# Last tokens' low parts on VectorE, a projection between halves of the modulation's matmuls, and a second modulation group on VectorE

## The chip, the cores and the metric

The kernel runs on one core of a Trainium2 chip. The metric is device time in microseconds. The kernel before took 2394.74 us (median of three executions, 2394.31 to 2396.17). A core has TensorE (matmuls; PE in the profile, its weight loads PEld), VectorE (DVE), ScalarE (ACT), GpSimd (POOL) and SyncE (SP, which issues the DMAs here). Each runs its own queue in order; semaphores join them.

## The reference, cut to what matters

Two layers of a diffusion backbone over 512 latent and 128 context tokens, 1024 wide. Each token's normalised input is scaled and shifted by a modulation that is computed from a conditioning vector and a large matrix `w_mod` (1024 x 6144 for each layer); there are two conditioning vectors, one for latent and one for context tokens.

```python
mod = matmul(silu(cond), w_mod) + b_mod
sh1, sc1, ga1, sh2, sc2, ga2 = split(mod, 6)
h = rmsnorm(x, g_pre1) * (1 + sc1) + sh1
proj = matmul(h, w_in)                 # 12 pieces: four mixers' inputs and the gates
br = einsum('btmc,mcd->btmd', branches, w_br)   # a, b, c, d: attention, MLA, pooling, gated DeltaNet
mix = matmul(sum(sigmoid(gate) * br), w_o)
x = x + ga1 * rmsnorm(mix, g_post1)
h2 = rmsnorm(x, g_pre2) * (1 + sc2) + sh2
gt, up = split(matmul(h2, w_up), 2)
x = x + ga2 * rmsnorm(matmul(silu(gt) * up, w_down), g_post2)
```

## The kernel before

The 640 tokens are five tiles of 128 (`NT` is 5): tiles 0 to 3 latent, tile 4 context. Nearly every matmul is done in three products of rounded halves: an operand v is split into a high part (ScalarE copies it to the rounded type) and a low part (v minus the high part, a subtraction of two SBUF operands, on VectorE or GpSimd); then high x high, high x low and low x high go into one PSUM bank. Weights come in chunks through `wchunk` (lines 139 to 150 for the call): DMA into `raw`, ScalarE makes `whi`, VectorE makes `wlo` at line 150. All matmuls of this kind are recorded at line 134, transposes at line 139.

A scheduler with priorities orders each engine's queue when the kernel is built; `after` and `keep` bind one instruction behind another on the same engine; pools of named slots (`V` 2, `P` 4, `U` 4, `raw`, `whi`, `wlo` 3 each) and PSUM banks (`psg` 3, `pss` 2, `psc`, `pst`, `pso` 1 each) make a later user wait for the earlier one. So an edit at one place can move instructions at others.

Layer 0 fills the span up to about 1205 us, its feed-forward from about 760; layer 1 follows, its feed-forward from about 1940. What the change touches:

*The normalised tile before the feed-forward.* `prenorm` transposes tile i, scales it (line 371 on VectorE, 369 on ScalarE), and then, for the feed-forward, `norm_blocks` makes the parts by halves q of the model width. High parts come from ScalarE at line 1280; the low part of half 0 is on GpSimd, that of half 1 on VectorE, both at line 1282. The tokens go to two blocks of 320 tokens; `U` holds both parts of a block's first half, `hhi`/`hlo` those of its second half. `combine` (line 1293 and its ScalarE copies at 1297) then makes sums of blocks, into `X` and `T`, for a scheme that saves one of the products of the up projection. Ahead of the attention layers, `prenorm` itself makes the parts (line 377), in the same split of engines.

*The first projection.* At the start of layer 0 the modulation itself (`first_norm`, line 417, 32 matmuls for a chunk of 256 columns of shift and scale, small moving operand, weights straight from DMA) and the projection `proj_tm` run together: a chunk's modulation, and then the projection of the chunk before it, for five token tiles, six products each.

*The other modulation groups.* A group is 2048 columns of `w_mod`. `mod_group` does one on TensorE (line 207, 32-column weights, blocks from `V`), as a generator `bg` that the gates and projections of a layer advance. `mod_group_v` does one on VectorE: 64 multiply-adds of 128x512 (line 308 the first of an accumulator, line 310 the others, 8 DMAs for each of 4 accumulators of tag `P`), then 8 matmuls with a selecting matrix and `mod_finish`, with 4 transposes. It is the feed-forward's `filler`; `step()` advances it by one piece (two DMAs, four multiply-adds). Layer 0 has groups 1 and 2 on TensorE; for layer 1, group 0 is the filler in layer 0's feed-forward, and groups 1 and 2 are on TensorE in layer 1.

*The feed-forward.* `ffn` takes the 22 blocks of hidden columns in six groups (`FGROUPS`); in each, up projections of pairs of blocks, the gating, the split of the hidden values into `U`, and a `w_down` pass whose results are added into `acc` and `oh` at line 1472. Products of transformed operands bring subtractions at line 1323.

## Time and profile before

| | |
|---|---|
| median of three | 2394.74 us |
| the profiled execution | 2396.94 us |
| its span, first to last instruction | 2395.1 us |
| mean granted TensorE clock | 0.989 |
| PE busy | 2291.1 us (96%) |
| PEld busy | 2020.9 us (84%) |
| DVE busy | 1577.0 us (66%) |
| ACT busy | 984.2 us (41%) |
| POOL busy | 280.5 us (12%) |
| DMA, mean over the span | 113 GB/s |

Busy times are summed for each engine over the span. A timeline row has the start of an instruction, its duration, the engine, the line of the kernel, the operation with the tile it writes and those it reads, partitions by elements, and in brackets how long the engine had been idle before it and which engine's result ended that. Durations of neighbours overlap, so what one costs in a run of equal ones is the distance between their starts. A row marked x4 stands for four such instructions in sequence. A row of the windows view has a stretch, its length, the busy time of PE, PEld, DVE, ACT and POOL in it with the count of instructions, the granted TensorE clock, the busy share of the DMA engines and GB/s. A granted clock of 1.00 is 2.4 GHz, 0.50 is 1.2 GHz.

### The profile page before, as it was taken

The page shows a single profiled execution, that of the slowest core. Times are in us where ns is not written, and L with a number is a line of the kernel's source. Part 1 is how long each engine was busy: PE and PEld are TensorE (multiplying, and loading weights), DVE is VectorE, ACT ScalarE, POOL GpSimd, SP SyncE. Part 2 cuts the span into 40 slices and gives each one's busy share as a digit, 9 for nine tenths or more (in the row PEclk, how much of TensorE's full clock was granted, in tenths as well). Part 3 has the DMA queues.
Part 4 walks back from the last instruction along what each step waited for, and adds up shares of the span by engine and source line. Part 5 has one row for each costly group of instructions (what it writes and reads, how often), then busy time and mean ns, then how long its engine had stood idle before and what let it go on. Part 6 is the DMA issues. An engine that isn't in the chain of part 4 may idle for free. (4 is left out here: it accounts for less than half of the span.)

```text
span 2395.1 us, 38984 instructions
## 1 busy us (share of the span) xinstructions
PE 2291.1 (96%) x15094; PEld 2020.9 (84%) x15094; DVE 1577.0 (66%) x3370; ACT 984.2 (41%) x2046; POOL 280.5 (12%) x326
## 2 busy tenths in 40 slices
PE   7999999999999899999989999999999979999998
PEld 5877678989887889998878776889798869999997
DVE  5562787567357898666766538884763577667667
ACT  3351444233226534433564424532322355334433
POOL 0100113223022100000020002031310320000001
PEclk9999999999999999999999999999999989999999
DMA  8637213414434344222452561334253432223223
GB/s 263 168 118 214 68 58 99 126 51 111 134 127 140 98 134 141 78 71 93 121 154 73 157 205 30 99 85 100 60 137 124 129 123 71 88 72 106 71 89 114
DMA packets 328330, 269.48 MB, mean 113 GB/s; under 512 B 71552, under 2 KB 287232, under 8 KB 328144
## 3 DMA queue, kind: packets, MB, share of 16 engines
q1 hardware_dynamic: 328144, 266.98, 37.4%
q8 instruction: 119, 1.95, 0.3%
q14 instruction: 67, 0.55, 0.1%
HBM read 234.73 MB, written 32.20 MB: 111 GB/s over the span
## 5 line engine op out<-in xcount | busy, mean ns | idle before, releaser
L134 PE MATMUL psg<-hhi,whi 128*128 128x384 f32 (+2 forms) x1648 | 515.9, 320 | 11.7 <-DVE tg L1175 5.6
L134 PE MATMUL psg<-hhi,wlo 128*128 128x384 f32 (+2 forms) x1648 | 512.7, 318 | 2.2 <-DVE wlo L150 2.0
L134 PE MATMUL psg<-hlo,whi 128*128 128x256 f32 (+2 forms) x1568 | 504.0, 321 | 0.1
L150 DVE TENSOR_TENSOR wlo<-raw,whi 128x1024 fp32r<-128x1024 f32 (+1 forms) x176 | 219.5, 1248 | 208.2 <-ACT whi L149 205.5
L134 PEld LDWEIGHTS psg<-hhi,whi 128*128 128x128 f32 x1648 | 310.7, 190 | 22.9 <-DVE tg L1175 7.1
L134 PEld LDWEIGHTS psg<-hhi,wlo 128*128 128x128 f32 x1648 | 310.8, 190 | 15.5 <-issue 9.3
L134 PEld LDWEIGHTS psg<-hlo,whi 128*128 128x128 f32 x1568 | 298.2, 190 | 15.6 <-issue 13.2
L149 ACT ACTIVATE whi<-raw 128x1024 fp32r<-128x1024 f32 (+1 forms) x176 | 185.7, 1057 | 225.1 <-PE psg L134 166.6
L1144 ACT ACTIVATE tg<-psg 128x384 f32<-128x384 f32 (+1 forms) x128 | 54.9, 431 | 222.0 <-PE psg L134 203.1
L1337 ACT ACTIVATE wlo<-raw 128x512 fp32r<-128x512 f32 x120 | 75.8, 632 | 158.2 <-PE psc L134 91.4
L1323 DVE TENSOR_TENSOR wlo<-raw,wlo 128x512 fp32r<-128x512 f32 x120 | 82.8, 690 | 64.8 <-ACT wlo L1337 64.2
L134 PE MATMUL pss<-hhi,whi 128*128 128x320 f32 x504 | 122.9, 309 | 0.0
L134 PE MATMUL pss<-hhi,wlo 128*128 128x320 f32 x504 | 122.7, 308 | 0.0
L134 PE MATMUL psg<-oh,whi 128*128 128x384 f32 (+1 forms) x512 | 117.7, 315 | 3.8 <-DVE tg L1175 3.5
L134 PE MATMUL psg<-whi,U 128*128 128x512 f32 x356 | 118.7, 393 | 1.8 <-DVE U L157 1.3
L1177 POOL TENSOR_TENSOR acc<-acc,tg 128x640 f32<-128x640 f32 x48 | 85.3, 1780 | 241.8 <-DVE tg L1175 241.8
L1488 POOL TENSOR_TENSOR acc<-acc,oh 128x512 f32<-128x512 f32 x8 | 11.3, 1409 | 814.4 <-ACT dt L1487 808.4
L1323 DVE TENSOR_TENSOR whi<-raw,whi 128x512 fp32r<-128x512 f32 x120 | 82.3, 689 | 33.9 <-ACT whi L1337 33.9
L134 PE MATMUL pss<-whi,U 128*128 128x512 f32 x304 | 102.4, 391 | 0.8 <-DVE cv L1323 0.8
L134 PEld LDWEIGHTS psg<-oh,whi 128*128 128x128 f32 x512 | 85.0, 188 | 14.2 <-DVE tg L1175 6.9
L1337 ACT ACTIVATE whi<-raw 128x512 fp32r<-128x512 f32 x120 | 75.4, 631 | 41.5 <-DVE raw L1323 27.4
L134 PEld LDWEIGHTS pss<-hhi,whi 128*128 128x128 f32 x504 | 87.3, 188 | 0.0
(578 smaller groups left out, 5114.6 us busy)
## 6 DMA issues: line engine op xcount, KB each, us to landing
raw<-in_w_up SPq DMA_DIRECT2D x88, 512.0 KB, 3.6
raw<-in_w_in SPq DMA_DIRECT2D x86, 512.0 KB, 3.8
V<-in_w_mod SPq DMA_DIRECT2D x64, 512.0 KB, 4.7
raw<-in_w_down SPq DMA_DIRECT2D x44, 512.0 KB, 3.7
raw<-in_w_o SPq DMA_DIRECT2D x16, 512.0 KB, 3.8
V<-in_w_mod SPq DMA_DIRECT2D x32, 256.0 KB, 2.7
xs<-V SPq DMA_DIRECT2D x15, 512.0 KB, 3.4
V<-xs SPq DMA_DIRECT2D x15, 512.0 KB, 3.5
```

The lines of the kernel that those rows point to most:

```text
L134: return self.nc.tensor.matmul(out, lhsT, rhs, start=start, stop=stop, skip_group_check=True)
L149: nc.scalar.activation(hi, raw[:, :a * b], AF.Copy)
L150: nc.vector.tensor_tensor(lo, raw[:, :a * b], hi, op=ALU.subtract)
L1144: self.nc.scalar.activation(tg[:, o:o + sz], p, AF.Tanh, scale=0.5)
L1177: nc.gpsimd.tensor_tensor(a, a, tg, op=ALU.add)
L1323: tt = lambda o, x, y, op: nc.vector.tensor_tensor(o, x, y, op=op)
L1337: nc.scalar.activation(hi, src, AF.Copy)
L1488: nc.gpsimd.tensor_tensor(y, y, G[0 if i < 4 else 1][:, 0:512], op=ALU.mult)
```

## The change

Three edits. First, in `prenorm` and `norm_blocks` the low part of half 0 is on GpSimd for tiles 0 to 2 only; for tiles 3 and 4 it is on VectorE. Second, in `proj_tm` a chunk's modulation matmuls are bound in two halves; the previous chunk's projection of tile 0 stands between the halves, that of tile 1 behind the second, ahead of the transpose. Third, group 1 of layer 1's modulation goes from TensorE in layer 1 to VectorE in layer 0's feed-forward, behind group 0, and `step()` is called once more for each chunk of `w_down`.

```diff
--- before.py
+++ after.py
@@ -373,7 +373,7 @@
             if which:
                 continue
             nc.scalar.activation(hh[0][:, ks, sl], h32[:, ks], AF.Copy)
-            eng = nc.gpsimd if q == 0 else nc.vector
+            eng = nc.gpsimd if q == 0 and i < 3 else nc.vector
             eng.tensor_tensor(hh[1][:, ks, sl], h32[:, ks], hh[0][:, ks, sl], op=ALU.subtract)
         if which:
             self.norm_blocks(i, h32, hh)
@@ -515,17 +515,21 @@
         if norm:
             for c in range(4):
                 mods = next(norm)
+                n = len(mods) // 2
                 if prev:
                     self.after(mods[0], prev[-1])
                 chs[c] = self.tm_chunk(l, c)
                 tr = next(norm)
                 if c:
+                    prev.append(mods[n - 1])
+                    part(c - 1, range(1))
+                    self.after(mods[n], prev[-1])
                     prev.append(mods[-1])
-                    part(c - 1, range(1))
+                    part(c - 1, range(1, 2))
                 self.after(tr, prev[-1] if prev else mods[-1])
                 prev.append(tr)
                 if c:
-                    part(c - 1, range(1, NT))
+                    part(c - 1, range(2, NT))
             part(3, range(NT))
         else:
             for c in range(2):
@@ -1278,7 +1282,7 @@
                 hi, lo = hb[3 * q if second else 1 + q]
                 v = h32[:, 4 * q:4 * q + 4, src]
                 nc.scalar.activation(hi[:, :, dst], v, AF.Copy)
-                eng = nc.gpsimd if q == 0 else nc.vector
+                eng = nc.gpsimd if q == 0 and i < 3 else nc.vector
                 eng.tensor_tensor(lo[:, :, dst], v, hi[:, :, dst], op=ALU.subtract)
 
     def combine(self, i, h32, hb):
@@ -1462,6 +1466,7 @@
                     ps = [self.ps(b) for b in ("ssctg" if half == 0 else "ggssc")]
                     for k in range(0, nf, 2):
                         ch = mk(k, co)
+                        step()
                         for i in range(NT):
                             self.tmm(ps[i], ch, (0, 1), hs, (k, k + 1), i, k == 0, k == nf - 2)
                     for i in range(NT):
@@ -1533,7 +1538,7 @@
             br = {}
             br[2] = self.mixer_c(l, hh, L)
             br[0] = self.mixer_a(l, hh, L, tm)
-            self.bg = chain(*(self.mod_group(M, g, "c", "c") for g in (1, 2)))
+            self.bg = chain(*(self.mod_group(M, g, "c", "c") for g in ((1, 2) if l == 0 else (2,))))
             G = self.gdn_scalars(L, ab)
             if l == 0:
                 zt = self.t("X", [128, 2 * SLOT])
@@ -1568,7 +1573,7 @@
             if l + 1 < DEPTH:
                 Mn = self.mod_begin(l + 1)
 
-                filler = self.mod_group_v(Mn, 0, "o", "t")
+                filler = chain(*(self.mod_group_v(Mn, g, "o", "t") for g in range(2)))
             nh = self.new_h() if l + 1 < DEPTH else None
             dst = x_mid(1) if l + 1 < DEPTH else y_out
             self.ffn(l, hh, head, M, Mn, x_mid(0), dst, nh, filler)
```

VectorE, just before the feed-forward of layer 0, tile 4 (`P_7752`; `U_7105` and `U_7106` are the high and low part of its first half, `hhi_7103` and `hlo_7104` of the second). In the changed kernel lines behind the projection are 4 higher, those behind `step()` in the `w_down` pass 5. Before:

```order
L1293 TENSOR_TENSOR X_7851<-P_7889,X_7851 128x4x64
L1293 TENSOR_TENSOR T_7853<-P_7889,T_7852 128x4x64
L1293 TENSOR_TENSOR P_7929<-P_7929,hlo_7104 128x512
L1293 TENSOR_TENSOR P_7976<-P_7752,hhi_7103 128x512
L1282 TENSOR_TENSOR hlo_7104<-P_7752,hhi_7103 128x4x128
L1293 TENSOR_TENSOR hlo_7104<-P_7929,hhi_7103 128x4x128
L1293 TENSOR_TENSOR P_7929<-P_7685,P_7929 128x512
```

After:

```order
L1297 TENSOR_TENSOR X_7851<-P_7889,X_7851 128x4x64
L1297 TENSOR_TENSOR T_7853<-P_7889,T_7852 128x4x64
L371 TENSOR_SCALAR P_7752<-psc_7767,modA_235,modB_236 128x128
L1297 TENSOR_TENSOR P_7929<-P_7929,hlo_7104 128x512
L1286 TENSOR_TENSOR U_7106<-P_7752,U_7105 128x4x128
L1286 TENSOR_TENSOR hlo_7104<-P_7752,hhi_7103 128x4x128
L1297 TENSOR_TENSOR hlo_7104<-P_7929,hhi_7103 128x4x128
L1297 TENSOR_TENSOR P_7929<-P_7685,P_7929 128x512
L1297 TENSOR_TENSOR P_7976<-P_7752,hhi_7103 128x512
```

The low part `U_7106` stands ahead of `hlo_7104`, behind one operation of the combining; the first operation on `P_7976` moved behind them. The low part of tile 3 entered the queue in the same way, ahead of these rows.

TensorE at the start of layer 0, second chunk (`psc` holds the modulation, `psg_238` the projection of tile 0, `psg_239` that of tile 1, of the first chunk's weights `whi_296`, `wlo_297`; the second three products of a tile, on the other half of the chunk, are left out). Before:

```order
L417 MATMUL psc_315<-acc_316,cs_218 32x128 x8
L417 MATMUL psc_315<-T_327,cs_218 32x128 x8
L417 MATMUL psc_315<-U_338,cs_218 32x128 x8
L417 MATMUL psc_315<-acc_349,cs_218 32x128 x8
L134 MATMUL psg_238<-whi_296,hhi_74 128x496
L134 MATMUL psg_238<-wlo_297,hhi_74 128x496
L134 MATMUL psg_238<-whi_296,hlo_75 128x496
...
L139 MATMUL pst_368<-cst_63,oh_243 128x128
```

After:

```order
L417 MATMUL psc_315<-acc_316,cs_218 32x128 x8
L417 MATMUL psc_315<-T_327,cs_218 32x128 x8
L134 MATMUL psg_238<-whi_296,hhi_74 128x496
L134 MATMUL psg_238<-wlo_297,hhi_74 128x496
L134 MATMUL psg_238<-whi_296,hlo_75 128x496
...
L417 MATMUL psc_315<-U_338,cs_218 32x128 x8
L417 MATMUL psc_315<-acc_349,cs_218 32x128 x8
L134 MATMUL psg_239<-whi_296,hhi_74 128x496
...
L139 MATMUL pst_368<-cst_63,oh_243 128x128
```

Sixteen modulation matmuls stand now behind tile 0's products, and tile 1's stand ahead of the transpose.

VectorE in the feed-forward of layer 0, end of the up projections of the fourth group of blocks and start of its `w_down` additions (`P_10342` is an accumulator of modulation group 1, `V` a piece of `w_mod`). Before:

```order
L150 TENSOR_TENSOR wlo_10216<-raw_10213,whi_10215 128x1024
L157 TENSOR_TENSOR U_10121<-tg_9846,U_10120 128x640
L157 TENSOR_TENSOR U_10121<-tg_9847,U_10120 128x640
L1323 TENSOR_TENSOR dt_10295<-raw_10291,raw_10293 128x512
L1323 TENSOR_TENSOR raw_10291<-raw_10291 128x4x128
L150 TENSOR_TENSOR wlo_10252<-raw_10249,whi_10251 128x1024
L1472 TENSOR_TENSOR acc_8023<-acc_8023,pss_10126 128x512
L1472 TENSOR_TENSOR acc_8024<-acc_8024,pss_10127 128x512
L1472 TENSOR_TENSOR acc_8025<-acc_8025,psc_10128 128x512
```

After:

```order
L150 TENSOR_TENSOR wlo_10339<-raw_10336,whi_10338 128x1024
L157 TENSOR_TENSOR U_10228<-tg_9952,U_10227 128x640
L157 TENSOR_TENSOR U_10228<-tg_9953,U_10227 128x640
L310 SCALAR_TENSOR_TENSOR P_10342<-V_10391,cs_218,P_10342 128x512 x2
L310 SCALAR_TENSOR_TENSOR P_10342<-V_10558,cs_218,P_10342 128x512
L1327 TENSOR_TENSOR dt_10435<-raw_10431,raw_10433 128x512
L310 SCALAR_TENSOR_TENSOR P_10342<-V_10558,cs_218,P_10342 128x512
L1327 TENSOR_TENSOR raw_10431<-raw_10431 128x4x128
L310 SCALAR_TENSOR_TENSOR P_10342<-V_10562,cs_218,P_10342 128x512
L1477 TENSOR_TENSOR acc_8023<-acc_8023,pss_10233 128x512
L150 TENSOR_TENSOR wlo_10384<-raw_10381,whi_10383 128x1024
L1477 TENSOR_TENSOR acc_8024<-acc_8024,pss_10234 128x512
```

Multiply-adds of the filler stand now between the splits of hidden values and weights and the additions, where there were none.

## Rows read from the trace of the kernel before

**Rows 1.** windows: four stretches (columns as told above)
```profile
840.00:900.00 60.00, 58.78 (x333) 53.68 (x334) 54.94 (x89) 22.92 (x42) 0.00 (x0) 1.00 0.45 138
900.00:960.00 60.00, 58.24 (x363) 55.45 (x363) 49.34 (x79) 26.31 (x48) 0.00 (x0) 1.00 0.45 144
960.00:1020.00 60.00, 60.00 (x377) 57.58 (x376) 39.84 (x64) 27.83 (x52) 0.00 (x0) 1.00 0.23 71
1400.00:1410.00 10.00, 10.00 (x83) 8.62 (x82) 2.82 (x6) 1.82 (x3) 0.21 (x1) 1.00 0.85 257
```

**Rows 2.** timeline of PE, ahead of both feed-forwards
```profile
781.00 0.52 PE L134 MATMUL psg<-U,whi 128*128 128x320 f32 x1 [2.48 <-ACT U L1280]
781.32 0.47 PE L134 MATMUL pss<-U,whi 128*128 128x320 f32 x1
781.59 0.47 PE L134 MATMUL psg<-U,whi 128*128 128x320 f32 x1
787.77 0.64 PE L134 MATMUL psg<-U,whi 128*128 128x320 f32 x1 [5.71 <-POOL U L1282]
...
1964.28 0.31 PE L134 MATMUL psg<-U,whi 128*128 128x320 f32 x1
1970.65 0.63 PE L134 MATMUL psg<-U,whi 128*128 128x320 f32 x1 [6.05 <-POOL U L1282]
```

**Rows 3.** timeline of POOL before the feed-forward of layer 0
```profile
777.44 1.28 POOL L1282 TENSOR_TENSOR U<-P,U 128x512 fp32r<-128x512 f32 x1 [15.11 <-ACT U L1280]
781.03 6.69 POOL L1282 TENSOR_TENSOR U<-P,U 128x512 fp32r<-128x512 f32 x1 [2.31 <-ACT U L1280]
```

**Rows 4.** timeline of DVE, same stretch
```profile
781.10 0.68 DVE L1293 TENSOR_TENSOR P<-P,hhi 128x512 f32<-128x512 f32 x1
781.70 0.68 DVE L1282 TENSOR_TENSOR hlo<-P,hhi 128x512 fp32r<-128x512 f32 x1
...
794.54 0.69 DVE L1293 TENSOR_TENSOR X<-P,X 128x512 fp32r<-128x512 f32 x1 [7.95 <-ACT X L1297]
```

**Rows 5.** windows: three stretches with a lowered clock
```profile
30.90:36.80 5.90, 5.90 (x24) 4.47 (x25) 2.10 (x6) 2.58 (x4) 0.00 (x0) 0.50 1.08 375
787.70:791.30 3.60, 3.53 (x13) 3.53 (x14) 0.00 (x0) 0.00 (x0) 0.01 (x1) 0.50 0.00 0
1970.60:1974.10 3.50, 3.45 (x13) 3.45 (x14) 0.00 (x0) 0.00 (x0) 0.00 (x0) 0.50 0.00 0
```

**Rows 6.** timeline of DVE and of PE, first projection
```profile
28.00 0.82 DVE L443 TENSOR_TENSOR hlo<-X,hhi 128x640 fp32r<-128x640 f32 x1
...
30.89 1.07 PE L417 MATMUL psc<-acc,cs 128*32 128x128 f32 x12 [0.49 <-DMA acc<-in_w_mod]
```

**Rows 7.** windows, line 207 alone, layer 1 (length, PE, PEld, PEclk, DMA, GB/s)
```profile
1382.00:1425.50 43.50, 9.41 (x128) 2.83 (x128) 1.00 0.79 241
```

**Rows 8.** timeline of PE, end of the second modulation group of layer 1
```profile
1424.34 0.64 PE L207 MATMUL psc<-V,cs 128*32 128x256 f32 x8
1424.91 0.44 PE L134 MATMUL psg<-hlo,whi 128*128 128x384 f32 x1
1425.19 0.34 PE L134 MATMUL psg<-hhi,wlo 128*128 128x384 f32 x1
1425.37 0.34 PE L134 MATMUL psg<-hhi,whi 128*128 128x384 f32 x1
```

**Rows 9.** timeline of DVE, first addition of three w_down passes, layer 0
```profile
956.15 0.68 DVE L1472 TENSOR_TENSOR acc<-acc,pss 128x512 f32<-128x512 f32 x1
...
1032.64 0.68 DVE L1472 TENSOR_TENSOR acc<-acc,pss 128x512 f32<-128x512 f32 x1
...
1111.68 0.68 DVE L1472 TENSOR_TENSOR acc<-acc,pss 128x512 f32<-128x512 f32 x1
```

**Rows 10.** lines of DVE, the filler: count, busy us, mean ns, idle before
```profile
L310 DVE SCALAR_TENSOR_TENSOR P<-V,cs,P 128x512 f32<-128x512 f32 x56 | 40.5, 751 | 3.5 <-DMA V<-in_w_mod 3.4
L308 DVE TENSOR_SCALAR P<-V,cs 128x512 f32<-128x512 f32 x8 | 3.7, 487 | 2.2 <-DMA V<-in_w_mod 2.2
```

## The prediction

> **What bounds the kernel.** I read the busy shares first, then tables of busy time by stretch, and then the order of single instructions on each engine around the edited places. TensorE is busy 96% of the span, VectorE 66%, ScalarE 41% (the table above). So the time is TensorE's matmul time plus its idle pieces plus what a lowered clock costs, and an edit is worth only what it takes out of those three. The stretches differ: from 1400 to 1410 us (layer 1, where modulation matmuls are mixed into other work) and from 960 to 1020 us (feed-forward of layer 0) TensorE is busy to the full, VectorE 2.8 of 10 and 39.8 of 60. From 840 to 960 us, where the feed-forward of layer 0 already carries one modulation group on VectorE, VectorE is at 54.94 and 49.34 of 60 and TensorE loses 1.22 and 1.76 us [rows 1]. The reader is to keep two things: TensorE has no slack to hide an added matmul, and VectorE has slack in some stretches only.
>
> **(a) Low parts of the last two token tiles on VectorE.** Before the feed-forward, TensorE needs the first half of the normalised last tile as a high part (ScalarE) and a low part (GpSimd). In layer 0 it starts on the high part at 781.00, runs three products, and then waits 5.71 us for the low part; in layer 1 it waits 6.05 us, until 1970.65 [rows 2]. The row on GpSimd shows why: the same subtraction of 128x512 took 1.28 us for tile 3 and 6.69 us for tile 4 [rows 3]. What differs is VectorE beside it: there operations of 0.68 us stand back to back, one every 0.60 us, until 786.59 (the row at 794.54 began after 7.95 us of idleness), not stretched [rows 4]. GpSimd ended 1.13 us after VectorE's run did.
>
> The Trainium skill ("SBUF — State Buffer", section "Who interferes with whom") says that a VectorE instruction with two SBUF inputs and a GpSimd instruction that reads SBUF exclude each other, and that whichever starts first keeps the ports until it ends. By that rule GpSimd, once started, would have been done in about 1.3 us and VectorE would have paused; the rows show the opposite, so the measurement decides. By the rule TensorE would lose under 1 us there, and this part would be worth about 1 us, not 12.
>
> In the new order (first pair of pieces above) the subtraction stands on VectorE at the place where, in the old one, the operation of 781.10 stood. So in layer 0 it runs from about 781.10 to 781.78. TensorE would come to it at 781.59 + 0.27 = 781.86, against 787.77: 5.9 us gone. In layer 1 TensorE runs at full clock there (384 columns take 0.18 us from start to start [rows 8], so these 320 about 0.15) and comes to the low part at 1964.28 + 0.15 = 1964.43; on VectorE it can be done about 0.32 us later, one slot of 0.60 us behind a high part that comes as TensorE starts. So 1964.75 against 1970.65: 5.9 us gone and 0.3 us of wait left. After each wait the clock was 0.50 (its 1.2 GHz level) for 3.6 and 3.5 us [rows 5], so at most 1.8 + 1.75 us more come back. But in layer 0 the products stood 0.27 us apart already after the 2.48 us gap ahead of 781.00 [rows 2], which stays. I take half, 1.75 us.
>
> The cost: VectorE runs two operations of 0.60 us more per layer, ahead of a chain that ends 7.95 us before VectorE's next one. This idle time hides them; what TensorE needs next from that chain it reads only after twelve more products on data that are there. If that cover fails, it costs 1.2 us a layer. The line at the end of layer 0 (two subtractions moved for the next projection) is worth nothing by my reading, 0.7 us either way at most (one such operation). Sum of (a): 5.9 + 5.9 + 1.75 = **-13.6** (bounds -16 and -10).
>
> **(b) The first projection.** TensorE's matmuls of chunks 1 to 3 keep their number; six projection matmuls go between the halves of a chunk's 32 modulation matmuls, and six more after them, ahead of the transpose (second pair). It pays where TensorE waits for a weight DMA in the second half: one such wait is 0.49 us at 30.89. The projection's high operand is there early, the low one comes at 28.82 [rows 6]; TensorE would come to it about there, so little is gained in chunk 1. Against it stands one more switch between the two kinds of matmul for each chunk, at 0.2 to 0.3 us (the working of a switch stands in (c)), for three chunks 0.8. The clock is 0.50 from 30.90 to 36.80 [rows 5]; if the earlier large matmuls raise it earlier by a third of that, 1 us comes back, if it rises at the start of the next chunk instead, as much is lost. I take **-0.5**: 0.5 + 0.8 saved (the wait and some of the clock), 0.8 paid; bounds -2.2 and +1.
>
> **(c) One more modulation group on VectorE.** *Removed:* in layer 1, 128 matmul records of group 1, 9.41 us busy [rows 7]. Their records overlap: eight take 0.64 us by the row, 0.57 us from start to start, so 9.41 x 0.57 / 0.64 = 8.4. They stand in 12 stretches; from 1424.34 to 1425.37 one stretch and two large products take 1.03 us, against 0.57 + 2 x 0.18 = 0.93: 0.1 for the switch back, and I take as much for the switch there, so 12 x 0.2 = 2.4. That is **-10.8** where TensorE is busy 10 of 10 [rows 1, 8]. Idle time for DMAs there I leave out.
>
> *Added:* in the feed-forward of layer 0, group 1's finish on TensorE (8 selecting matmuls, 4 transposes). Its price can be read from the first addition of each w_down pass: 956.15 to 1032.64 is 76.49 us, 1032.64 to 1111.68, with group 0's finish in it, 79.04 [rows 9]: **+2.55**. And 64 instructions on VectorE, 40.5 + 3.7 us busy for group 0 [rows 10]. They are spread by the order between the operand splits (third pair); group 0 now ends about where it did, and group 1 follows, about 955 to 1080 us. There VectorE has 60 - 39.84 = 20 us free per 60 us, so about 40 us go into 40 us of room: VectorE becomes as full as it was at 840 to 900. What the fullness costs TensorE is bounded below by nothing and above by twice the worst stretch (2 x 1.76 us in 60, so some 7 over 120 us); the nearest row is group 0's, 1.22 + 1.76 = **+3.0** over its 120 us [rows 1], which I take (bounds 0 and +7). Each of these instructions waits for a DMA of 256 KB into one of two slots; behind it on VectorE stand the low parts of weights and the low parts of hidden blocks, for which TensorE waits. Group 0 paid 3.5 + 2.2 us of VectorE idleness for those DMAs [rows 10], inside the 3.0. Group 1's first accumulator needs a slot that group 0's selecting matmuls release; I put that wait at under 0.4 us, in the 3.0 as well. The new DMAs on SP's queue stand between weight loads in a stretch that had moved 71 GB/s, against 257 at 1400 to 1410 [rows 1], so the loads do not crowd.
>
> Sum of (c): -10.8 + 2.55 + 3.0 = **-5.2** (bounds -8.3 and -1.2).
>
> **All:** -13.6 - 0.5 - 5.2 = **-19.3**. The profiled execution took 2396.94 us, so 2377.6 of its own kind; it lay 2.2 us over the median of 2394.74, by which the prediction is **2375.4**.
>
> **Rivals.**
> *The filler saturates VectorE (slower).* VectorE runs in order, so once it has no room, each filler instruction pushes a weight's low part, and TensorE waits. For: 54.94 of 60 already at 840 to 900 with one group at work [rows 1]. Against: at 960 to 1020, where group 1 goes, it is 39.84. If group 1's whole 40.5 us [rows 10] were exposed, (c) is -10.8 + 2.55 + 40.5 = +32 and the time about 2394.7 - 14.1 + 32 = 2413. It decides over the sign from the point where TensorE's added idle time passes 3.0 + 19.3 = 22 us, half the filler. The Trainium skill ("Perfetto Trace Analysis", section "Optimizing Scalar/DVE Operations") says that with a saturated VectorE work is better moved off it, to ScalarE or even GpSimd; by that both (a) and (c) go the wrong way. The trace agrees on fullness at 840 to 900 only.
> *The wait in (a) is taken over.* The subtraction stands in VectorE's chain of 0.60 us steps; were it some five steps later than I place it (for instance because an operation ahead of it waits for a slot), TensorE would wait about 3 us a layer for VectorE instead of 6 for GpSimd: 2375.4 + 6 = 2381. For: the low part sits in the middle of that chain. Against: the order puts only one of the combining operations that start after 780.5 ahead of it.
> *The removal in layer 1 does not pay.* If those matmuls only fill time in which TensorE would wait for weights or for gating results, (c) is +5.5 and the time 2394.7 - 14.1 + 5.5 = 2386. For: the stretch moves 257 GB/s, the DMA engines 0.85 busy [rows 1]. Against: the group's own DMAs go too, and TensorE shows no gap there.
>
> **How the numbers follow.** Chances: main forecast 0.78 (own range 2368 to 2383), VectorE saturated 0.05, wait taken over 0.09, removal without effect 0.08. The range that should hold 8 in 10 reaches over the two middle rivals: **2367 to 2387**. A change under 0.2% (4.8 us) cannot be told from none in this kernel. Faster than 2389.9: 0.97 of the main case, all of the second rival, over half of the third: 0.90. Within 0.2%: 0.06, from the tails of the main case and of the two others. Slower: 0.04, from the saturated VectorE.
>
> **What would show it.** (a) right: no wait of TensorE for the low part over 0.5 us ahead of either feed-forward, and no GpSimd row of 6 us; wrong: a wait there put down to VectorE. (b) right: the first 60 us shrink or grow by under 2 us. (c) right: TensorE still without gaps from 1370 to 1430, that stage shorter by about 11 us; in the feed-forward of layer 0 a second pass of about 79 us and TensorE's busy time at 58 to 59 of 60 until about 1080. The prediction is wrong if TensorE drops under 57 of 60 there, or if layer 1 ahead of its feed-forward shrinks by less than 6 us.

## The result and the profile after

The changed kernel took 2375.52 us (median of five, 2373.31 to 2381.14), the kernel before beside it 2396.17 (five, 2394.31 to 2402.15): a ratio of 0.9917, 95% interval 0.9898 to 0.9935. The forecast was 2375.4, range 2367 to 2387. The profiled execution was the longest of the five, 2381.14 us, its span 2379.3.

Busy times of the profile after:

```profile
PE 2288.7 (96%) x14982; PEld 2018.2 (85%) x14982; DVE 1611.6 (68%) x3440; ACT 983.5 (41%) x2046; POOL 260.3 (11%) x320
```

TensorE has 112 records less, VectorE 35 us more, GpSimd 20 us less; TensorE's busy time fell by 2.4 us only, since the disturbance told of below adds to it. Most of the gain is idle time that went (104.0 us before, 90.6 after), and that is read at the places.

*Ahead of both feed-forwards.* The timeline of PE after, to hold beside [rows 2]:

```profile
782.10 0.63 PE L134 MATMUL psg<-U,whi 128*128 128x320 f32 x1 [2.14 <-ACT U L1284]
782.53 0.47 PE L134 MATMUL pss<-U,whi 128*128 128x320 f32 x1
782.80 1.15 PE L134 MATMUL psg<-U,whi 128*128 128x320 f32 x2
...
784.01 0.73 PE L134 MATMUL psg<-U,whi 128*128 128x320 f32 x2
...
1955.01 0.31 PE L134 MATMUL psg<-U,whi 128*128 128x320 f32 x1
1955.85 0.40 PE L134 MATMUL psg<-U,whi 128*128 128x320 f32 x1 [0.54 <-DVE U L1286]
```

In layer 0 the low part's product is the second of the x2 at 782.80. The pair takes 1.15 us where a pair that waits for nothing takes 0.73 (784.01), so some 0.4 us of wait are left; in layer 1 one of 0.54 us is left, put down to VectorE. VectorE's row for it in layer 0:

```profile
782.51 0.69 DVE L1286 TENSOR_TENSOR U<-P,U 128x512 fp32r<-128x512 f32 x1
```

It starts 0.41 us after TensorE's first product of the high part and takes 0.69 us; on GpSimd the same work had ended 6.69 us after its start [rows 3]. The granted clock behind the wait was 0.50 before in the stretches of 3.6 and 3.5 us of [rows 5]; read in steps of half a microsecond it was 0.50 for 10.2 us around each of the two waits, in layer 1 until 1975.7 and not 1974.1. The windows view after (PE, PEld, DVE, ACT, POOL busy, PEclk, DMA share, GB/s):

```profile
785.00:789.00 4.00, 4.00 (x18) 4.00 (x17) 4.00 (x8) 1.27 (x2) 0.00 (x0) 0.53 0.00 0
787.70:791.30 3.60, 3.60 (x23) 3.60 (x23) 2.19 (x4) 1.88 (x4) 0.00 (x0) 0.86 0.02 5
1956.30:1960.00 3.70, 3.70 (x17) 3.70 (x17) 3.70 (x8) 1.26 (x2) 0.00 (x0) 0.57 0.00 0
```

It still falls, only earlier and for less long (6.8 us in layer 0 and 3.4 in layer 1 in this trace, 3.4 in both when the kernel ran again), and part of that cost stays.

*First projection.* The same view of the kernel after, against 0.50 from 30.90 to 36.80 [rows 5]:

```profile
30.00:32.00 2.00, 2.00 (x36) 1.18 (x35) 0.00 (x0) 0.00 (x0) 0.00 (x0) 0.76 1.01 318
32.00:34.00 2.00, 2.00 (x10) 1.66 (x11) 0.67 (x4) 1.15 (x2) 0.00 (x0) 1.00 1.09 383
34.00:36.00 2.00, 2.00 (x11) 1.67 (x10) 1.83 (x4) 2.00 (x4) 0.00 (x0) 1.00 1.09 384
```

TensorE is at 2.4 GHz from about 31 us on, and the DMA wait of 0.49 us [rows 6] is gone.

*Feed-forward of layer 0*, to hold beside [rows 1]:

```profile
840.00:900.00 60.00, 58.90 (x336) 53.78 (x335) 54.02 (x87) 21.28 (x38) 0.00 (x0) 1.00 0.48 149
900.00:960.00 60.00, 57.70 (x359) 52.57 (x358) 49.98 (x81) 26.65 (x49) 0.00 (x0) 1.00 0.43 133
960.00:1020.00 60.00, 59.75 (x374) 56.91 (x373) 55.87 (x98) 26.26 (x51) 0.00 (x0) 1.00 0.42 126
1020.00:1080.00 60.00, 56.22 (x303) 50.12 (x302) 50.65 (x82) 19.51 (x36) 0.00 (x0) 0.97 0.47 146
```

TensorE loses 2.30 us between 900 and 960 (1.76 before) and 3.78 between 1020 and 1080, where it lost nothing before (the row below). That is more than predicted: 56.22 of 60 is under the 57 that the prediction named as a sign that it is wrong. When the changed kernel ran again it was 58.02, with (c) alone 57.38. The last stretch before:

```profile
1020.00:1080.00 60.00, 60.00 (x345) 55.30 (x345) 41.44 (x65) 24.39 (x43) 0.00 (x0) 1.00 0.25 80
```

The first additions of the four w_down passes after, against [rows 9]:

```profile
874.82 0.68 DVE L1477 TENSOR_TENSOR acc<-acc,pss 128x512 f32<-128x512 f32 x1
...
954.56 0.68 DVE L1477 TENSOR_TENSOR acc<-acc,pss 128x512 f32<-128x512 f32 x1
...
1036.01 0.68 DVE L1477 TENSOR_TENSOR acc<-acc,pss 128x512 f32<-128x512 f32 x1
...
1117.67 1.45 DVE L1477 TENSOR_TENSOR acc<-acc,pss 128x512 f32<-128x512 f32 x2
```

From the first to the fourth it is 242.85 us; before it was 232.69 (878.99 to 1111.68). In layer 1, where no filler runs, three passes take 3 x 76.49 = 229.47 in both kernels. With a finish at 2.55 each (two after, one before), 0.67 us of waits before stand against 8.3 after. Of the 8.3 some 1.7 are a lowered clock, 0.50 for 3.4 us behind TensorE's wait at 1026.68 (shown with the experiments).

*Layer 1.* The 128 records of group 1 are gone. By rows of ScalarE that both traces have, the stretch from 1301 to 1522 us before is 13.0 us shorter after.

*A disturbance.* Laying those rows side by side shows one stretch where the kernel after lost 6.7 us: around 550 us, which the change does not touch. Windows view of after:

```profile
540.00:544.00 4.00, 3.44 (x15) 2.46 (x16) 4.00 (x11) 2.18 (x8) 2.28 (x3) 0.87 0.01 4
544.00:548.00 4.00, 4.00 (x12) 2.32 (x10) 1.25 (x3) 1.27 (x3) 3.31 (x4) 0.50 0.00 0
548.00:552.00 4.00, 4.00 (x15) 3.06 (x14) 1.75 (x5) 0.00 (x0) 0.00 (x0) 0.50 0.00 0
```

TensorE works without a pause there at 0.50. The waits ahead of it are the same, to 0.3 us, in traces of other kernels below in which the clock stayed at 1.00, so I do not count it to the change. The clock was 0.50 for 13.6 us in all. Without that this execution would lie near 2374.5 by estimate.

### The profile page after: what moved, and what is told of

Read it like the earlier page. It is cut to its first block, busy times and chain, and to the rows that moved or that the text cites. A ratio compares the mean times of both kernels' runs of the same rounds, so it can differ in the third digit from the quotient of the medians.

```text
span 2379.3 us, 38859 instructions
## 1 busy us (share of the span) xinstructions
PE 2288.7 (96%) x14982; PEld 2018.2 (85%) x14982; DVE 1611.6 (68%) x3440; ACT 983.5 (41%) x2046; POOL 260.3 (11%) x320
## 5 line engine op out<-in xcount | busy, mean ns | idle before, releaser
L310 DVE SCALAR_TENSOR_TENSOR P<-V,cs,P 128x512 f32<-128x512 f32 x112 | 81.2, 750 | 9.5 <-DMA V<-in_w_mod 9.5
```

What stands on the lines that cost most here:

```text
L310: nc.vector.scalar_tensor_tensor(acc[:, s, :], raw, self.cs[:, k, s:s + 1], acc[:, s, :], op0=ALU.mult, op1=ALU.add)
```

## The experiments

Each part alone first; then the kernel with group 1 done twice, then the cause of the waits, and last a version that goes further.

**Part (a) alone**, in `prenorm` and in `norm_blocks`

```diff
-            eng = nc.gpsimd if q == 0 else nc.vector
+            eng = nc.gpsimd if q == 0 and i < 3 else nc.vector
```

> The kernel before with part (a) alone. Theory: the two waits of TensorE for GpSimd's low part go (5.9 us each), half the lowered clock behind them comes back, and the low parts at the end of layer 0 give about 2 us more, so 13 to 15 us less than before. Rival: part of what the whole change shows at these places comes from the scheduler's new order with (b) and (c) in it; then (a) alone gives 10 us or less. If VectorE's chain took the wait over, 6 to 8 us.

Measured: 2379.48 us against 2394.64, ratio 0.9929 (0.9905 to 0.9953). Its trace against before, by rows of TensorE and ScalarE that both have: 6.5 us gained ahead of layer 0's feed-forward (1.1 of that given back inside it), 2.4 us at the end of layer 0, 0.9 lost again in layer 1 between 1300 and 1435, 6.8 us gained ahead of layer 1's feed-forward. So (a) makes most of the gain, by itself and at its own places. The rival with 10 us or less is out, and so is the wait that VectorE would have taken over.

**Part (b) alone**

```diff
+                n = len(mods) // 2
...
                 if c:
+                    prev.append(mods[n - 1])
+                    part(c - 1, range(1))
+                    self.after(mods[n], prev[-1])
                     prev.append(mods[-1])
-                    part(c - 1, range(1))
+                    part(c - 1, range(1, 2))
...
                 if c:
-                    part(c - 1, range(1, NT))
+                    part(c - 1, range(2, NT))
```

> The kernel before with part (b) alone. Theory: the whole gain comes by 40 us of the span, about 3 us, because TensorE's clock rises earlier (it was 0.50 from 30.9 to 36.8), and nothing of it is lost later. Rival, the prediction's size: 0.5 us, the rest of the 3 us in the whole change came from a DMA that landed earlier by chance; then the stretch up to 60 us is within 1 us of before.

Measured: 2394.43 us against 2394.64, ratio 0.9996 (0.9983 to 1.001): in the time it can't be told from nothing. In the trace the kernel is 2.2 us ahead at 92 us; the two kernels without (b), (a) alone and (c) alone, are 0.4 ahead there. Windows of (b) alone, and then of (a) alone, which has not (b):

```profile
30.00:32.00 2.00, 2.00 (x9) 1.13 (x12) 0.00 (x0) 0.00 (x0) 0.00 (x0) 0.50 1.05 341
32.00:34.00 2.00, 2.00 (x37) 1.67 (x38) 0.29 (x1) 1.03 (x1) 0.00 (x0) 1.00 1.08 376
34.00:36.00 2.00, 2.00 (x11) 1.66 (x10) 1.30 (x4) 1.04 (x2) 0.00 (x0) 1.00 1.09 382
```

```profile
30.00:32.00 2.00, 1.91 (x28) 1.00 (x20) 0.00 (x0) 0.00 (x0) 0.00 (x0) 0.50 0.98 308
32.00:34.00 2.00, 2.00 (x7) 1.61 (x6) 0.29 (x1) 1.03 (x1) 0.00 (x0) 0.50 1.09 383
34.00:36.00 2.00, 2.00 (x7) 1.56 (x6) 0.83 (x3) 0.57 (x1) 0.00 (x0) 0.51 1.09 383
```

The clock is up between 29 and 32 us in the ten traces of kernels with (b) and between 35.9 and 37 in the four without, those of the experiments below included. At the row of ScalarE that starts at 87.62 us before, the ten are 2.2 to 4.3 us ahead, the three others 0.1 to 0.4. So the mechanism is as the theory has it, 2 us and more.

**Part (c) alone**

```diff
-            self.bg = chain(*(self.mod_group(M, g, "c", "c") for g in (1, 2)))
+            self.bg = chain(*(self.mod_group(M, g, "c", "c") for g in ((1, 2) if l == 0 else (2,))))
...
-                filler = self.mod_group_v(Mn, 0, "o", "t")
+                filler = chain(*(self.mod_group_v(Mn, g, "o", "t") for g in range(2)))
...
                         ch = mk(k, co)
+                        step()
```

> The kernel before with part (c) alone. Theory from the trace of the whole change: layer 1 loses about 13 to 14 us, the feed-forward of layer 0 grows by 10 to 11 us (2.55 of it the finish on TensorE, the rest waits of TensorE for VectorE and a lowered clock), so 2 to 4 us less than before in all. Rival, the prediction's sizes: 10.8 less and 5.5 more, so 5 us less.

Measured: 2389.73 us against 2394.64, ratio 0.9977 (0.9963 to 0.999). In the trace the feed-forward of layer 0 grew by 10.2 us between 848 and 1083, and layer 1 lost 13.2 us. Two terms larger than predicted, with a difference of about the predicted size.

**Group 1 on both engines**

```diff
-            self.bg = chain(*(self.mod_group(M, g, "c", "c") for g in ((1, 2) if l == 0 else (2,))))
+            self.bg = chain(*(self.mod_group(M, g, "c", "c") for g in (1, 2)))
```

> The changed kernel in which layer 1 still does group 1 on TensorE as well (its result is the same as the one that VectorE made). It tells the price of the group on TensorE from that of the group on VectorE: the feed-forward of layer 0 should stay as in the changed kernel, first additions of the w_down passes some 81 us apart; layer 1 up to its feed-forward should be longer than in the changed kernel by 13 to 14 us if the removal is worth what the trace of the whole change shows, by 11 us if it is worth what was predicted.

Measured: 2387.19 us in one run. The same two operations of ScalarE, in the changed kernel and then in this one:

```profile
1357.91 0.32 ACT L681 ACTIVATE a_st<-lc,a_st 128x1 f32<-128x1 f32 x1
...
1596.51 0.49 ACT L1148 ACTIVATE tg<-psg 128x384 f32<-128x384 f32 x1 [6.96 <-PE psg L134]
```

```profile
1350.12 0.32 ACT L681 ACTIVATE a_st<-lc,a_st 128x1 f32<-128x1 f32 x1
...
1602.83 0.49 ACT L1148 ACTIVATE tg<-psg 128x384 f32<-128x384 f32 x1 [8.47 <-PE psg L134]
```

238.60 us against 252.71, so 14.1 us. The last 1.5 of them are not the group's: they lie in the 19 us ahead of the last row, where the clock of this trace fell to 0.50 for 3.4 us and that of the changed kernel did not. That stretch takes 18.6 or 17.1 us in every trace, with the group on TensorE and without (18.7 before and with (a) alone, 17.1 with (b) alone and with (c) alone). So the group costs 12.6 us on TensorE in layer 1. The prediction's 10.8 was the matmuls with their switches; it left out the idle times for their DMAs on purpose and the group's finish by oversight. These make some 1.2 of the 1.8 us between: TensorE's waits for V at line 207 in layer 1 are 1.0 us here and 0.2 in the changed kernel, and the four transposes of the finish start 0.11 us apart. The feed-forward of layer 0, which has the same instructions as in the changed kernel, lost 5.7 us to waits in this run, not 8.3.

The next four ask why the filler costs TensorE 8.3 us in the changed kernel, not 3. In the trace after, VectorE's idle times that end with a DMA stand ahead of TensorE's waits there:

```profile
1023.28 1.42 DVE L310 SCALAR_TENSOR_TENSOR P<-V,cs,P 128x512 f32<-128x512 f32 x2 [2.91 <-DMA V<-in_w_mod]
...
1062.93 0.69 DVE L1327 TENSOR_TENSOR dt<-raw,raw 128x512 f32<-128x512 f32 x1 [2.75 <-DMA raw<-in_w_up]
```

```profile
1026.68 0.50 PE L134 MATMUL pss<-whi,U 128*128 128x512 f32 x1 [1.81 <-DVE cv L1327]
...
1071.39 1.15 PE L134 MATMUL psg<-X,whi 128*128 128x320 f32 x6 [1.10 <-ACT oh L1362]
```

At 1023.28 the filler's operation waited 2.91 us for its piece of `w_mod`, in order, with the subtractions behind it for which TensorE then waited 1.81 us at 1026.68. At 1062.93 it was a weight load that came late; from there VectorE had no pause until 1073.6, and the copy of ScalarE for which TensorE waited at 1071.39 stood behind an operation that had waited 0.74 us for VectorE. So besides a full VectorE there are two more suspects: the filler's DMAs and slots, and SP's queue, in which weight loads stand behind pieces that wait for a slot (SP's waits from 950 to 1120 after: total us, times, longest):

```profile
SPq L305 <- DVE P L310: 54.2, 26, 5.0
SPq L1323 <- DVE raw L1327: 20.4, 4, 6.5
```

**Fewer DMAs, all of VectorE's work**

```diff
-                raw = self.t("V", [128, SLOT])[:, :512]
-                c = g * 2048 + j * 512
-                self.dma.dma_start(raw, I["w_mod"][l, k * 128:k * 128 + 128, c:c + 512])
+                if g == 0 or k == 0:
+                    raw = self.t("V", [128, SLOT])[:, :512]
+                    c = g * 2048 + j * 512
+                    self.dma.dma_start(raw, I["w_mod"][l, k * 128:k * 128 + 128, c:c + 512])
```

> The changed kernel in which group 1 of the filler loads one piece of w_mod for each accumulator instead of eight and uses it eight times: the same 64 operations on VectorE, 4 DMAs instead of 32 (so group 1's sums leave out seven eighths of the matrix). The stretch from the first addition of the second w_down pass in the feed-forward of layer 0 to that of the fourth was 155.5 us before, 163.1 us in the changed kernel, of which 2.55 is the finish. Theory (the waits come from SP's queue and the two slots: VectorE stands in order behind a late piece, and weight loads stand on SP behind a piece that waits for a slot): most of the 5 us of waits goes, the stretch takes 158 to 159.5 us. Rival (VectorE is too full): it stays at 162 to 163 us.

**All DMAs, half of VectorE's work**

```diff
-                for s in range(2):
+                for s in range(2 if g == 0 or k < 1 else 1):
```

> The changed kernel in which group 1 of the filler does the multiply-adds for the second conditioning vector with the first piece only: 36 operations on VectorE instead of 64, all 32 DMAs (the sums of the context tokens leave out seven eighths of the matrix). Theory of VectorE's fullness: the stretch of 163.1 us falls to 158 to 160 us. Rival, the DMAs and slots: it stays at 161.5 to 163 us, since the 32 DMAs still pass through two slots in order.

**The filler's DMAs on GpSimd's queue**

```diff
-                self.dma.dma_start(raw, I["w_mod"][l, k * 128:k * 128 + 128, c:c + 512])
+                nc.gpsimd.dma_start(raw, I["w_mod"][l, k * 128:k * 128 + 128, c:c + 512])
```

> The changed kernel with the filler's DMAs issued by GpSimd, idle in that stretch, instead of SP: no weight load stands behind a piece that waits for a slot. If the in-order queue of SP is the cause, the stretch of 163.1 us falls to 158 to 160.5 us, and the idle time of VectorE that ends with a load of in_w_up gets shorter; if VectorE's fullness or the two slots are, it stays at 162 to 164 us. GpSimd must make the descriptors itself, which could also be slower than SP: then VectorE waits longer for the pieces, and the stretch grows.

**Two pieces in one DMA**

```diff
-                raw = self.t("V", [128, SLOT])[:, :512]
                 c = g * 2048 + j * 512
-                self.dma.dma_start(raw, I["w_mod"][l, k * 128:k * 128 + 128, c:c + 512])
+                if k % 2 == 0:
+                    two = self.t("V", [128, SLOT])[:, :1024].rearrange("p (k c) -> p k c", k=2)
+                    self.dma.dma_start(two, I["w_mod"][l, k * 128:k * 128 + 256, c:c + 512].rearrange("(k p) c -> p k c", p=128))
+                raw = two[:, k % 2, :]
```

> The changed kernel with two pieces of w_mod loaded by one DMA of 512 KB into one slot: half the DMAs, and as much ahead in two slots as four pieces. If VectorE's waits for late pieces and SP's waits for slots are the cause, the stretch of 163.1 us falls to 158 to 161 us; if VectorE's fullness is, it stays at 162 to 164 us.

The kernels with 4 DMAs and with 36 operations leave out part of group 1's sums. Measured, from the first additions in each trace (waits: what is over 229.47 + 2 x 2.55 us, a lowered clock included), with VectorE's waits for pieces of `w_mod` from 780 to 1130 us and its busy time from 960 to 1080. The totals are single runs and are not compared; the kernel before took 2406.41 us beside the last four.

| kernel | one run, us | second to fourth | first to fourth | waits | VectorE's waits for pieces | VectorE busy, of 120 |
|---|---|---|---|---|---|---|
| changed kernel | 2381.14 | 163.11 | 242.85 | 8.3 | 12.2 | 106.52 |
| 4 DMAs for 32 | 2371.28 | 155.74 | 235.71 | 1.1 | 5.3 | 113.85 |
| 36 operations for 64 | 2373.99 | 156.79 | 237.43 | 2.9 | 13.2 | 97.66 |
| DMAs on GpSimd's queue | 2377.95 | 162.28 | 241.76 | 7.2 | 19.7 | 107.24 |
| two pieces a DMA | 2370.48 | 156.70 | 234.96 | 0.4 | 2.0 | 112.87 |

These are single traces, and other traces of the same filler show their spread: the changed kernel's has 8.3, 5.2 (the changed kernel again), 5.7 (group 1 on both engines) and 7.3 us ((c) alone), two pieces a DMA 0.4, 2.1, 0.6 and 1.2 (this run and the three timed kernels below). The two sets lie apart. The 7.2 us with GpSimd's queue lie inside the first.

The windows view settles it best, 960 to 1080 us of the kernel with 4 DMAs, and then of the one with two pieces a DMA:

```profile
960.00:1080.00 120.00, 120.00 (x738) 114.02 (x737) 113.85 (x187) 53.91 (x101) 0.00 (x0) 1.00 0.32 93
```

```profile
960.00:1080.00 120.00, 119.27 (x731) 113.03 (x730) 112.87 (x185) 53.22 (x100) 0.00 (x0) 1.00 0.46 141
```

With 4 DMAs VectorE is busy 113.85 of 120 us, fuller than in the same stretch of the changed kernel (106.52), and TensorE does not lose a hundredth. So a VectorE that is busy for 95% of the time does not by itself make TensorE wait. Whether SP's queue has a part is not settled: with GpSimd issuing, VectorE's waits for weight loads fell (15.4 to 10.0 us from 780 to 1130), but those for pieces rose (12.2 to 19.7), and TensorE lost as much. What costs is VectorE standing in order behind a late piece while it has no room to catch up. Take the lateness away (4 DMAs, two pieces a DMA) or the fullness (36 operations, with pieces as late as before) and most of the waits go. Two pieces a DMA is at once fewer DMAs and more data ahead in the two slots; no run tells these apart. The expectations had it as one or the other; both of their ranges were too high (155.7 and 156.8 us against 158 and more), because they had group 0's finish in the stretch from the second to the fourth addition, and it stands ahead of it at 950 us. Half of VectorE's work helped nearly as much as an eighth of the DMAs, which the pure DMA theory did not allow.

**A version that beats both**

> The changed kernel once more, beside the two kernels below on the same chip, so that they are compared with it and not only with the kernel before: about 20 us less than before by every theory.

> The changed kernel with two pieces of w_mod in one DMA, timed. Its single run had the three w_down passes of layer 0's feed-forward 7.9 us shorter than the changed kernel (234.96 against 242.85 us from the first to the fourth first addition). If that is what it is worth, it takes 7 to 9 us less than the changed kernel, 27 to 29 less than before; if it only moved the waits to another place, less than 3.

The third, beside them, has in both places of part (a)

```diff
-                eng = nc.gpsimd if q == 0 and i < 3 else nc.vector
+                eng = nc.vector
```

> As the run before, and the low parts of tiles 0 to 2 on VectorE too, so that GpSimd makes none. Theory from part (a): the row of 6.69 us came where VectorE worked without a pause beside GpSimd; the other tiles' operations of 1.3 us delay nobody, so this changes nothing beyond 1 to 2 us (two waits of 1.0 and 0.4 us for GpSimd at line 377 go). Rival: VectorE, with four operations of 0.60 us more before each feed-forward and eight at line 377, now delays TensorE: 2 to 5 us slower than the run before.

| kernel | median, us | lowest to highest | ratio to before (interval) |
|---|---|---|---|
| changed kernel again | 2377.65 | 2372.83 to 2384.64 | 0.9922 (0.9893 to 0.9951) |
| two pieces a DMA | 2364.94 | 2364.70 to 2369.80 | 0.9871 (0.9847 to 0.9896) |
| the same, no low part on GpSimd | 2366.26 | 2365.54 to 2373.41 | 0.9879 (0.9851 to 0.9908) |

Two pieces a DMA is the best kernel here: 8.1 us below the changed kernel by the fastest runs, as expected, 12.7 by the medians, and its longest run (2369.80) is below the other's shortest. Of the 12.7, about 7.7 us lie between 490 and 620 us, where the changed kernel's trace has the same lowered clock as its first one and this kernel's has not, which is luck as far as is known; the feed-forward of layer 0 gives 5.8, and 2.0 are lost near 1850 us. The intervals against before touch, so the size of the gain is uncertain: some 5 us by these two traces without that stretch, 8.1 by the fastest runs. Taking the other tiles off GpSimd changes nothing that can be told.

**The same without (b)**

The edit of (b) above is undone in the kernel with two pieces a DMA.

> The kernel with two pieces in one DMA (2364.94 us) with part (b) undone: the projection follows all of a chunk's modulation matmuls again. Theory: TensorE's clock is at 0.50 until about 36 us again instead of 31, and the stretch up to 60 us and the whole are 2 to 3 us longer: 2367 to 2368 us. Rival: what (b) gives at the start is lost again later, as the time of (b) alone might say, which is not told apart from none: 2364 to 2366 us, though the stretch up to 60 us is longer.

Measured: 2369.48 us (2364.21 to 2382.90), ratio 0.9905 (0.9876 to 0.9933). In the trace it is 3.0 us behind at 103 us and 4.5 at the end, so what (b) gives at the start is not taken back. Its runs spread over nearly 19 us, its fastest is below every run of the kernel with (b); the time doesn't tell the two apart. Shown is the early rise of the clock; that (b) shortens the kernel by 2 to 3 us is what the traces say and the medians don't contradict.

## Why the prediction was right

The sign, the time and the share of (a) came out. Three terms were too small, (b) and both of (c), and their errors nearly cancelled. That the forecast lies 0.1 us from the median is luck: when the same kernel ran again its median was 2377.65. Two of the prediction's own signs of being wrong came up in size: TensorE at 56.22 of 60 where 57 was the line for (c), and the first 60 us shorter by 3.0 where 2 was the line for (b) (2.0 when it ran again). The wait of 0.54 us in layer 1 is just over the line of 0.5 for (a).

- *Bound by TensorE, gain only from its idle time.* Right: [rows 1, 2] named the places, and parts alone gained at those places.
- *(a), 5.9 + 5.9 + 1.75 = 13.6.* Right: 13.9 in the trace of (a) alone, 15.2 in its time. Ahead of the feed-forwards it was 6.5 and 6.8: the waits for the low part fell by 5.37 and 5.51 to 0.34 and 0.54, the waits for the high part by some 0.35 each, and the remaining 0.8 and 0.9 fit the clock, which was 0.50 for 10.2 us around each wait before and for 3.4 with (a) alone. That is about the half that was taken, though [rows 5] do not show the lowered clock whole: their second stretch ends before it did. The end of layer 0, priced at nothing with 0.7 either way, gave 2.4 us. About 0.7 of that are the places where TensorE waited for GpSimd's last low parts before; about 1.5 come from a clock of 0.50 for 3.4 us near 1209 before, which the trace of (a) alone lacks and that of the changed kernel has again, so they are luck. A wait there for a weight's low part is 1.62 us before and 1.73 with (a) alone. In exchange 1.1 us were lost again in the feed-forward and 0.9 between 1300 and 1435. The order of the queues placed the subtraction to within half a microsecond.
- *(b), -0.5 with bounds -2.2 and +1.* The mechanism was there, the size was not: 2.2 us for (b) alone, 3.2 in the whole change and 2.2 when that ran again, of which 0.4 are seen without (b) too. The term that failed is the clock's, "if the earlier large matmuls raise it earlier by a third of that": it rose earlier by some 5 of the 5.9 us.
- *(c), removal at -10.8.* Mis-sized by some 2 us: 12.6 (group 1 on both engines) to 13.2 us (c alone). Left out were idle times for DMAs, 0.8 us, and the finish in layer 1, some 0.4; what the rest is stays open.
- *(c), waits at +3.0 on the finish's 2.55.* Mis-sized: the three passes grew by 10.2 us (9.2 with (c) alone, 7.6 with group 1 on both engines, 7.1 when the changed kernel ran again), so 4.6 to 7.6 for waits, with a bound of 7. The step that failed is that group 1's stretch had "about 40 us into 40 us of room" and so would be like group 0's: the room was used up (55.87 of 60 us from 960 to 1020), and then late pieces counted, 12.2 us of them in that trace. Group 0's 3.5 + 2.2 us of VectorE's idleness for DMAs [rows 10] were in the rows; what was missed is that they stop being free when VectorE has nothing left to catch up with.
- *The rivals.* A saturated VectorE, as a mechanism by itself, is refuted up to the fullness that was reached: 113.85 of 120 us with TensorE at 120.00. As one of two conditions it is part of what happened. The wait in (a) was not taken over beyond 0.54 us. The removal paid in full.
- *Sum.* -13.9 - 2 - 4 ((c) alone: 13.2 less, 9.2 more) is -20 in the parts alone; by their times -15.2, -0.2 and -4.9. The whole change measured -20.65 by medians. The parts add up; what differs between the two readings of (b) is open within the spread of the runs.

What stays open: why the clock falls for 13.6 us near 550 us in both traces of the changed kernel and not in those of its variants, with the same waits ahead of it; six of the other traces have a fall of 3.4 us between 530 and 548. It is worth 6 to 8 us, more than (b) or (c).

## What to carry to other kernels

Where an engine off the bound makes the last operand before a stage, look at what runs beside it: a row five times as long as its sister's names the place and the price. Work moved to an engine with "room" is priced by its operands' arrival as much as by its busy time: in an in-order queue a late DMA costs little while there is slack (13.2 us of lateness cost 2.9 here) and much when there is none (10.4 to 12.8 us cost 5.2 to 8.3), so make the data arrive earlier with the move, here by bigger pieces in the same slots. And a sum that comes out right can hide terms that are wrong: run the parts alone, and read the clock at each place in more than one trace before a microsecond or two is put down to an edit.

## What the hardware showed that was not expected

- The Trainium skill ("SBUF — State Buffer", section "Who interferes with whom") was said in the prediction to be contradicted by the row of 6.69 us. More rows speak for it. Where GpSimd began first, VectorE's operation was the one that grew; VectorE and then GpSimd, kernel after, end of layer 0:

```profile
1210.13 1.42 DVE L377 TENSOR_TENSOR hlo<-P,hhi 128x512 fp32r<-128x512 f32 x1
```

```profile
1209.71 1.29 POOL L377 TENSOR_TENSOR hlo<-P,hhi 128x512 fp32r<-128x512 f32 x1 [3.08 <-ACT hhi L375]
```

VectorE's subtraction takes 1.42 us for 0.68, as if it began when GpSimd's, at 1209.71 + 1.29 = 1211.00, was done. At 781.03 [rows 3] VectorE was in the middle of an operation, and each of the following began before the one ahead had ended (0.68 us long, 0.60 apart [rows 4]): GpSimd came in only when the run was over at 786.59, and its 6.69 us are the wait and then its own 1.1. Read so, the rule and the rows agree: what was wrong was to take the row's start for the start of its work. That is argued from these rows; no run was made for it. And another place shows that a run without a gap does not always keep GpSimd out; VectorE and then GpSimd, kernel before, end of layer 0:

```profile
1213.13 1.19 DVE L150 TENSOR_TENSOR wlo<-raw,whi 128x992 fp32r<-128x992 f32 x1
1214.23 1.79 DVE L377 TENSOR_TENSOR hlo<-P,hhi 128x512 fp32r<-128x512 f32 x1
```

```profile
1213.24 2.23 POOL L377 TENSOR_TENSOR hlo<-P,hhi 128x512 fp32r<-128x512 f32 x1 [7.50 <-DVE oh L1484]
```

GpSimd's row begins inside VectorE's first operation here too, and VectorE's second begins 0.09 us before the first has ended; yet GpSimd is done at 1215.47, 1.15 us after that first one, and it is VectorE's second that grows, to 1.79 us. So GpSimd's long rows are waiting, but when its turn comes stays open.

- The granted clock fell to 0.50 for 13.6 us near 550 us in two traces and not in others with the same waits (above), which makes these executions some 6 to 7 us longer. The mean granted clock goes with the times of the changed kernel's five later runs, which spread over 12 us: 0.993 in the two shortest, 0.991 in the traced one, 0.989 in the two longest. Where the clock fell in those without a trace is not known.
